# A decoder trunk of two layers: input laid out transposed, attention outputs stored already split

## The chip, the cores and the metric

The kernel runs on one core of one Trainium2 chip. The time is that of one execution on the device, in microseconds (us); where several runs are given, their median. A profile is one further execution, recorded by the hardware profiler: PE is TensorE (the matrix engine; PEld its weight loads), DVE VectorE, ACT ScalarE, POOL GpSimd, SP SyncE. SP, ACT and POOL also issue transfers (DMA), each in its own order; a trailing q (SPq) marks such a queue's work.

## The reference, cut to what matters

Two residual layers over 512 tokens of width 2048, all in float32.

```python
for i in range(DEPTH):                                  # DEPTH = 2
    hn = rms_norm(x, norm_w[i])
    if i % 2 == 0: out = diff_attention_mixer(hn, ...)  # layer 0
    else:          out, v_first = rwkv7_mixer(hn, ...)  # layer 1
    x = x + out

# layer 0: 8 heads, q and k as 2 x 128 a head, v and gate as 256
q, k, v, gate = split(h @ w_in, 4)                      # w_in: 2048 x 8192
q, k = rope(rms_norm(q, q_gain)), rope(rms_norm(k, k_gain))
a = softmax(q0 k0) - lam * softmax(q1 k1)               # causal
o = rms_norm(a @ v, subln_w) * (1 - lambda_init) * silu(gate)
out = o @ w_out                                         # w_out: 2048 x 2048
```

Layer 1 (RWKV-7) has a wide in-projection, a recurrent state per head that is computed in chunks, and an out-projection of the same size. Almost nothing of it is touched.

## The kernel before

**Split products.** Each float32 operand of a matmul is split into a rounded high part and the rest (names ending in H and L, or wh and wl). `mm3` (L119) multiplies a pair by three matmuls: H x H, H x L, L x H. `split_w` (L104 on ACT, L105 on DVE) makes wh and wl from a weight chunk of two K tiles, "K tile" being 128 of the 2048 channels that are summed over. wraw (the raw weights) has three buffers, wh and wl two each, so one chunk is split while PE uses the other. L561 are the same products in the form that heads 1 to 7 use, where sums of blocks save products.

**Layer 0, start.** x (tokens on partitions) is loaded on SP in slices of 128 or 256 channels, in an order by hand (`issue_after`, which puts an instruction behind another of the same engine), with the first weight tile on ACT's queue behind a load of the norm weights as 32 rows. These are turned by PE into columns (`load_rows`, L197, L199). `more` turns x's slices on PE, four transposes a K tile (L829) into PSUM, between the matmuls of `unit_tok`; `make_h` (L1059 on ACT, L1060 on DVE) scales the turned tile by the norm weights and splits it into one of the 16 K tiles hH, hL. 1/rms is applied later, from 16 squares of x on ACT (L841). Some matmuls of the identity (L796) run ahead of the first product. Tables for rope and lambda are made on DVE from small loads on SP.

**Layer 0, heads.** The unit of head h (h = 1 to 7) runs while the attention of head h - 1 goes along in it as a chain: after so many matmuls (`tick`) it issues its next step. `turn_y` ends it: the output block y (128 tokens x 256) is turned, scaled into yTh by two ACT operations (L410) and stored to the DRAM tensor yd (channels x tokens) by ACT's queue (L411). There are 28 of these; those of head 7 go straight into two K tiles (L416, L417).

**Layer 0, out-projection.** `split_rows` loads yd's first 14 row tiles on SP into yr (L458) and `split_row` splits each into a pair of the pool hp, which is where the in-projection's K tiles were (L448 on ACT, L449 on DVE). `unit_tok` uses them for the first two of four column blocks, while head 7's attention runs as a chain (L311: transposes of q and k). For the other two, `sum_forms` loads rows again, on POOL, into frow (L643) and forms sums of blocks (L649 on DVE), which are split into fS (L661 on ACT, L662 on DVE); `seven` multiplies them. `take` (L525) adds finished PSUM blocks on DVE. The same `split_rows` and `sum_forms` serve layer 1's out-projection, from the tensor yd2.

**Order.** The program is written with priorities (`high_priority`: weight splits and make_h ahead, steps of a chain further ahead), and the framework fixes each engine's order when it is built. Tiles with the same tag share buffers; a tile waits for the last reader of the one that was there.

Of the kernel before, what the change touches and what calls it, by code (L numbers as in the profile page):

```python
# [13 lines left out]
F32 = mybir.dt.float32  # L14
# [75 lines left out]
def split_w(g, parts, kg, cols, k0, raw=None, fine=False):  # L90
# [7 lines left out]
    for ks in [slice(k, k + 1) for k in range(kg)] if fine else [slice(0, kg)]:  # L98
        k = k0 + ks.start
        with ExitStack() as after:  # L100
            if raw is not None and parts and k < 4:
                for ins in g.made[k - 1] if k else [g.made_prm]:
                    after.enter_context(g.tc.issue_after(ins))
            nc.scalar.copy(hi[:, ks], raw[:, ks])  # L104
            nc.vector.tensor_sub(lo[:, ks], raw[:, ks], hi[:, ks].bitcast(F32))  # L105
# [54 lines left out]
def unit_tok(g, aH, aL, parts, cols, npp=NT, more=None, late=True):  # L160
# [6 lines left out]
    for k0 in range(0, KT, KG):  # L167
        raw, fine = g.first.pop(0) if g.first else (None, False)
        if fine:
            more(1, None)  # L170
        wh, wl = split_w(g, parts, KG, cols, k0, raw, fine)
# [3 lines left out]
        for i, (k, t) in enumerate(order):  # L175
            if more and (fine and i % 2 == 0 or i in (0, 2, 4)):
                more(1 + i // 2 if fine else k0 + (k + 1 + i % 4 // 2 if by_k else KG + i // 2), m)
            kk = k0 + k
            s = slice(t * P, (t + 1) * P)
            m = mm3(nc, pts[t][:, :cols], aH[kk][:, s], aL[kk][:, s], wh[:, k, :], wl[:, k, :],  # L180
                    kk == 0, kk == KT - 1, g)
    return pts


def fetch_rows(g, pieces, queue, tag="junk", bufs=2):
    t = g.tmpc.tile([P, P], F32, name="prow", tag=tag, bufs=bufs)
    for r0, n, ap in pieces:
        queue.dma_start(out=t[r0 : r0 + n, :], in_=ap)
    return t


def load_rows(g, pieces, rows, queue=None, t=None):

    nc = g.nc
    t = t or fetch_rows(g, pieces, queue)
    ps = g.ps.tile([P, 512], F32, name="prp", tag="pa", bufs=2)
    nc.tensor.transpose(ps[:, :rows], t[:rows, :], g.ident[:rows, :rows])  # L197
    o = g.const.tile([P, rows], F32, name=f"prm{pieces[0][2].tensor.name}")
    g.made_prm = nc.vector.tensor_copy(o[:], ps[:, :rows]).ins  # L199
    return o  # L200


def rope_tables(g, aps):
# [3 lines left out]
    nc.sync.dma_start(out=pos_i[:], in_=aps["positions"].rearrange("o (t p) -> (o p) t", p=P),)  # L207
# [3 lines left out]
    nc.sync.dma_start(out=inv[:], in_=aps["inv_freq"].partition_broadcast(P))  # L211
# [21 lines left out]
    for i, nm in enumerate(("da_q_gain", "da_k_gain")):  # L233
        gn = tmp.tile([P, P], F32, name="gain" + nm)
        nc.sync.dma_start(out=gn[:], in_=aps[nm][0].partition_broadcast(P))
# [8 lines left out]
def lambda_full(g, aps):  # L244
    nc = g.nc
    e = []
    for i in (1, 2):
        a = g.tmpc.tile([P, P], F32, name=f"lq{i}")
        b = g.tmpc.tile([P, P], F32, name=f"lk{i}")
        nc.sync.dma_start(out=a[:], in_=aps[f"da_lam_q{i}"][0].partition_broadcast(P))  # L250
        nc.sync.dma_start(out=b[:], in_=aps[f"da_lam_k{i}"][0].partition_broadcast(P))
# [90 lines left out]
def attention(g, h, qkT, qkL, sq, V, VL, G, gap, rows=None, keys=()):  # L342
# [58 lines left out]
    def turn_y(t):  # L401
# [5 lines left out]
        if rows is None:  # L407
            yT = w.tile([P, 2, P], F32, name="yTh", tag="yTh", bufs=1)
            for c in range(2):
                nc.scalar.activation(yT[:, c], pv[:, c], AF.Copy, scale=g.subw[:, c : c + 1])  # L410
            nc.scalar.dma_start(out=g.yd[h * 256 : (h + 1) * 256, ts].rearrange("(c p) t -> p c t", p=P), in_=yT[:])  # L411
            return
# [225 lines left out]
def sum_forms(g, src, i, rows, homes):  # L638
# [3 lines left out]
    for r, k0 in zip(rows, (i * KG, NS + i * KG)):  # L642
        nc.gpsimd.dma_start(out=r, in_=src[k0 * P : (k0 + KG) * P, :].rearrange("(k p) t -> p k t", p=P))  # L643
# [128 lines left out]
def layer0(g, aps):  # L772
# [3 lines left out]
    with ExitStack() as cx:  # L776
# [5 lines left out]
        def load_x(xt, cs, at):  # L782
            with tc.issue_after(g.last) if g.last else ExitStack():
                g.last = nc.sync.dma_start(
                    out=xt[:, :, at], in_=aps["x"][0, :, cs].rearrange("(t p) c -> p t c", p=P)).ins
# [13 lines left out]
        with tc.high_priority(offset=AHEAD):  # L799
            xs += [xp.tile([P, NT, 512], F32, name=f"x{cb}") for cb in range(4)]  # L800
            g.first += [(g.wraw.tile([P, 2, 512], F32, name="wraw", tag="wraw"), i == 0) for i in range(3)]
            at = lambda k, n: (xs[k // 4], slice(k * P, (k + n) * P), slice(k % 4 * P, (k % 4 + n) * P))
# [8 lines left out]
            load_x(*at(1, 1))  # L811
            load_first(0, slice(1, 2))
            load_x(*at(2, 1))
            load_first(2, slice(0, 2))
            load_x(*at(3, 1))
            load_x(*at(4, 2))
            load_first(4, slice(0, 2))
            for k in range(6, KT, 2):
                load_x(*at(k, 2))
# [3 lines left out]
        def more(n, m):  # L823
            for k in range(len(g.hH), min(n, KT)):
                ps = g.ps.tile([P, 512], F32, name="xT", tag="pa", bufs=2)
                cb, c0 = k // 4, k % 4 * P
                for t in range(NT):
                    with tc.issue_after(m.ins if m else warmed):
                        last = nc.tensor.transpose(ps[:, t * P : (t + 1) * P], xs[cb][:, t, c0 : c0 + P], g.ident[:])  # L829
# [892 lines left out]
```

## Time and profile before

| | |
|---|---|
| Runs before (median of 3) | 2156.53 us (2153.41 to 2157.34) |
| Profiled execution, its own time | 2158.04 us |
| Its span, first to last instruction | 2156.3 us |
| PE busy | 2118.2 us, 98% |
| DVE, ACT, POOL busy | 1604.7, 1137.2 and 357.5 us |
| Mean granted clock | 0.992 |
| Last `make_h` of layer 0 starts at | 962.9 us |

A row of a group gives line, engine, operation, output <- inputs, shapes and count, then busy time and the mean of one in ns, then the engine's idle time just before and what ended it. A row in order of time begins with start and length in us; the bracket holds the idle time before it and what released it. A row of waits gives total us, times, longest.

### The profile page before, as it was taken

The numbers are of one execution on the slowest core, as the hardware profiler recorded it, in microseconds if no ns is written. First come the engines' busy times: TensorE is split into PE (matmuls) and PEld (weight loads), VectorE is DVE, ScalarE is ACT, GpSimd is POOL, SyncE is SP. The second block draws the span as 40 slices with busy tenths as digits, with TensorE's granted clock in tenths as the row PEclk, the third lists the DMA queues.
The fourth block names the chain that finished last, engine by engine and source line by source line (L and its number), as shares of the span: only waits on it lengthen the run. The fifth ranks groups of instructions, "written<-read, shape, count | busy, mean of one in ns | idle before, by whom it ended". The sixth has DMA issues, their size and how long they took to land.

```text
span 2156.3 us, 34231 instructions
## 1 busy us (share of the span) xinstructions
PE 2118.2 (98%) x12008; PEld 1722.0 (80%) x12008; DVE 1604.7 (74%) x4091; ACT 1137.2 (53%) x2265; POOL 357.5 (17%) x720
## 2 busy tenths in 40 slices
PE   9999999999999999999999999999999999999999
PEld 8888888888888788878676887887888778777887
DVE  5997888878788884576667778877777788767645
ACT  6565555655556453355554555565555555645322
POOL 0010101011011100101222212222222122221001
PEclk9999999999999999999999999999999999999999
DMA  6566767677676756723222323323333232345565
GB/s 194 148 138 175 167 157 186 150 181 165 158 186 167 187 187 193 165 79 96 79 79 77 94 83 91 91 78 100 94 93 93 84 91 91 104 126 180 180 164 122
DMA packets 135953, 284.12 MB, mean 132 GB/s; under 512 B 47636, under 2 KB 63972, under 8 KB 135780
## 3 DMA queue, kind: packets, MB, share of 16 engines
q1 hardware_dynamic: 81296, 187.89, 27.5%
q0 software_dynamic: 21760, 75.77, 18.6%
q10 hardware_dynamic: 32724, 18.27, 2.8%
q8 instruction: 94, 1.54, 0.3%
q14 instruction: 79, 0.65, 0.1%
HBM read 261.89 MB, written 19.99 MB: 131 GB/s over the span
## 4 chain that ended last, share of the span: by engine, by line
PE 32%; DVE 14%; issue 4%; DMA 3%; ACT 2%; SPq 0%; POOL 0%; ACTq 0%; DVEq 0%; POOLq 0%
PE pp L119 19%; PE pt L119 5%; DVE tmpl L1331 3%; DVE Tm L1333 2%; DVE wl L105 2%; DMA td<-Tm 2%; DVE VS L1466 1%; PE gp L1267 1%; PE sm L1444 1%; PE sm L1462 1%; DMA TT<-td 1%; PE sm L1455 1%; PE px L1373 1%; PE px L1363 1%; DVE l L1216 1%
## 5 line engine op out<-in xcount | busy, mean ns | idle before, releaser
L105 DVE TENSOR_TENSOR wl<-wraw,wh 128x1024 fp32r<-128x1024 f32 (+2 forms) x305 | 371.1, 1217 | 224.4 <-ACT wh L104 210.3
L104 ACT CAST wh<-wraw 128x1024 fp32r<-128x1024 f32 (+2 forms) x305 | 318.3, 1044 | 333.8 <-PE pp L119 182.7
L119 PE MATMUL pp<-hH,wl 128*128 128x512 f32 x1024 | 416.3, 407 | 0.5 <-DVE wl L105 0.5
L119 PE MATMUL pp<-hL,wh 128*128 128x512 f32 x1024 | 415.9, 406 | 0.0
L119 PE MATMUL pp<-hH,wh 128*128 128x512 f32 x1024 | 413.5, 404 | 0.0
L119 PEld LDWEIGHTS pp<-hH,wh 128*128 128x128 f32 x1024 | 194.8, 190 | 36.0 <-issue 1.5
L119 PEld LDWEIGHTS pp<-hL,wh 128*128 128x128 f32 x1024 | 194.7, 190 | 35.1
L561 PE MATMUL pp<-wh,hH 128*128 128x512 f32 x560 | 221.6, 396 | 1.1 <-ACT wh L104 0.7
L119 PEld LDWEIGHTS pp<-hH,wl 128*128 128x128 f32 x1024 | 194.6, 190 | 33.4 <-DVE wl L105 0.9
L561 PE MATMUL pp<-wh,hL 128*128 128x512 f32 x560 | 218.7, 391 | 0.0
L561 PE MATMUL pp<-wl,hH 128*128 128x512 f32 x560 | 174.6, 393 | 0.0
L119 PE MATMUL pp<-wl,hH 128*128 128x512 f32 x372 | 146.1, 394 | 2.4 <-DVE wl L105 2.4
L119 PE MATMUL pp<-wh,hH 128*128 128x512 f32 x372 | 147.3, 397 | 0.8 <-DVE acc L525 0.8
L119 PE MATMUL pp<-wh,hL 128*128 128x512 f32 x372 | 146.5, 395 | 0.0
L1331 DVE SCALAR_TENSOR_TENSOR tmpl<-LT,Tm 128x60 f32<-128x60 f32 (+24 forms) x496 | 134.6, 271 | 10.9
L1450 POOL COPY SA<-VS 64x64 f32<-64x64 f32 x224 | 60.9, 272 | 459.7 <-DVE VS L1466 355.1
L561 PEld LDWEIGHTS pp<-wh,hH 128*128 128x128 f32 x560 | 105.2, 188 | 23.4 <-ACT G L265 1.3
L561 PEld LDWEIGHTS pp<-wh,hL 128*128 128x128 f32 x560 | 105.2, 188 | 21.2
L561 PEld LDWEIGHTS pp<-wl,hH 128*128 128x128 f32 x560 | 103.3, 188 | 21.6 <-DVE wl L105 0.5
L1333 DVE TENSOR_TENSOR Tm<-Tm,tmpl 128x60 f32<-128x60 f32 (+24 forms) x496 | 104.5, 211 | 11.2
L1457 ACT COPY VS<-sm 64x64 f32<-64x64 f32 x256 | 52.8, 206 | 64.2 <-PE sm L1455 59.3
L119 PEld LDWEIGHTS pp<-wl,hH 128*128 128x128 f32 x372 | 70.2, 189 | 16.0 <-DVE wl L105 2.7
(387 smaller groups left out, 4263.3 us busy)
## 6 DMA issues: line engine op xcount, KB each, us to landing
wraw<-in_rw_w_in_dram SPq DMA_DIRECT2D x128, 512.0 KB
wraw<-in_da_w_in_dram SPq DMA_DIRECT2D x92, 512.0 KB
wraw<-in_da_w_out_dram SPq DMA_DIRECT2D x26, 512.0 KB
wraw<-in_rw_w_out_dram SPq DMA_DIRECT2D x26, 512.0 KB
Ta<-in_da_w_in_dram POOLq DMA_DIRECT2D x21, 512.0 KB, 5.6
Tb<-in_da_w_in_dram POOLq DMA_DIRECT2D x21, 512.0 KB, 5.9
Tc<-in_da_w_in_dram POOLq DMA_DIRECT2D x21, 512.0 KB, 5.7
wraw<-in_da_w_in_dram POOLq DMA_DIRECT2D x21, 512.0 KB, 5.7
```

The lines of the kernel that those rows point to most:

```text
L104: nc.scalar.copy(hi[:, ks], raw[:, ks])
L105: nc.vector.tensor_sub(lo[:, ks], raw[:, ks], hi[:, ks].bitcast(F32))
L119: m = nc.tensor.matmul(out, a, b, start=s, stop=e, skip_group_check=skip)
L561: m = nc.tensor.matmul(out[t][:], x, wt[lo][:, k, :], start=first, stop=end and lo == 1 and k == KG - 1, skip_group_check=True)
L1216: nc.vector.tensor_tensor_scan(l[:].rearrange("p c t -> p (c t)"), g.rmask[:].rearrange("p c t -> p (c t)"), lw[:], 0.0, ALU.mult, ALU.add)
L1267: m = nc.tensor.matmul(gp[h][:, i * P : (i + 1) * P], BK[r_, c0 + i, :, :], p.AR[r_, c0 + i, :, :], start=True, stop=True)
L1331: nc.vector.scalar_tensor_tensor(tt, LT[:, i : i + 1, i + 1 :].to_broadcast([P, s, n]), n2[:, i : i + 1], Tm[:, 0:s, i : i + 1].to_broadca ...
L1333: nc.vector.tensor_add(Tm[:, 0:s, i + 1 :], Tm[:, 0:s, i + 1 :], tt)
L1363: nc.tensor.matmul(px[hi, c * HALF : (c + 1) * HALF], p.G[lo, c, 0, h, HALF:C], T1[lo, c, :], start=True, stop=True, tile_position=(b0, b0 ...
L1373: nc.tensor.matmul(px[lo, N + c * HALF : N + (c + 1) * HALF], X[hi, c, :], TT[hi, c, h, HALF:C], start=True, stop=True, tile_position=(b0 ...
L1450: nc.gpsimd.tensor_copy(p.SA[r_, c - 1, :], VS[r_, c, h, :])
L1457: nc.scalar.copy(VS[r_, c, h, :], sm[r_, P : P + C])
```

## The change

Five things. (1) The host also hands over x transposed, as xT with channels on partitions, and the norm weights and the RWKV constants as columns. `make_h` reads xT from SBUF; x itself is loaded later, for the squares, on ACT's queue. The hook is now `turn`, called by `split_w` after each split; `more` stays for the out-projections. Ten warm-up matmuls come ahead of the first product. (2) `rwkv_consts` loads three tensors as columns instead of rows that PE turns. (3) Small loads go on POOL instead of SP, and the mask is made on POOL first. (4) `turn_y` makes both parts of the output and stores them to yd, now of the shape (16, 128, 2, 512), in two stores; before the out-projection, the parts are loaded into tiles of hp with no split. (5) `sum_forms` loads yd's high part and adds the low part onto it with a second, adding load.

```diff
 def split_w(g, parts, kg, cols, k0, raw=None, fine=False, turn=None):
...
-            if raw is not None and parts and k < 4:
-                for ins in g.made[k - 1] if k else [g.made_prm]:
-                    after.enter_context(g.tc.issue_after(ins))
-            nc.scalar.copy(hi[:, ks], raw[:, ks])
-            nc.vector.tensor_sub(lo[:, ks], raw[:, ks], hi[:, ks].bitcast(F32))
+            for ins in g.made[-1] if turn and g.made else ():
+                after.enter_context(g.tc.issue_after(ins))
+            a = nc.scalar.copy(hi[:, ks], raw[:, ks])
+            d = nc.vector.tensor_sub(lo[:, ks], raw[:, ks], hi[:, ks].bitcast(F32))
+        if turn:
+            turn(ks.stop - ks.start, a.ins, d.ins)
...
 # turn_y
-            yT = w.tile([P, 2, P], F32, name="yTh", tag="yTh", bufs=1)
             for c in range(2):
-                nc.scalar.activation(yT[:, c], pv[:, c], AF.Copy, scale=g.subw[:, c : c + 1])
-            nc.scalar.dma_start(out=g.yd[h * 256 : (h + 1) * 256, ts].rearrange("(c p) t -> p c t", p=P), in_=yT[:])
+                yT = w.tile([P, 2, P], F32R, name="yTh", tag=("yTh", "th")[c], bufs=1)
+                nc.scalar.activation(yT[:, 0], pv[:, c], AF.Copy, scale=g.subw[:, c : c + 1])
+                nc.vector.scalar_tensor_tensor(yT[:, 1], pv[:, c], g.subw[:, c : c + 1],
+                                               yT[:, 0].bitcast(F32), ALU.mult, ALU.subtract)
+                nc.scalar.dma_start(out=g.yd[2 * h + c, :, :, ts], in_=yT[:].bitcast(F32))
...
 # sum_forms
-        nc.gpsimd.dma_start(out=r, in_=src[k0 * P : (k0 + KG) * P, :].rearrange("(k p) t -> p k t", p=P))
+        if len(src.shape) == 2:
+            nc.gpsimd.dma_start(out=r, in_=src[k0 * P : (k0 + KG) * P, :].rearrange("(k p) t -> p k t", p=P))
+            continue
+        for part, op in ((0, ALU.bypass), (1, ALU.add)):
+            nc.gpsimd.dma_start(out=r, in_=src[k0 : k0 + KG, :, part].rearrange("k p t -> p k t"),
+                                accum_op=op)
...
 # layer0, start
-            load_x(*at(0, 1))
-            warmed = warm_up(5)
-            g.prm_a = load_rows(g, [(0, 32, aps["norm_w"].rearrange("l (k p) -> (l k) p", p=P))], 32, nc.scalar)
-            first = load_first(0, slice(0, 1), nc.scalar)
+            g.prm_a = g.const.tile([P, 32], F32, name="norms")
+            first = nc.scalar.dma_start(out=xT[:, 0], in_=aps["xT"][:, 0]).ins
+            with tc.issue_after(first):
+                first = nc.scalar.dma_start(out=g.prm_a[:], in_=aps["norm_w"]).ins
+            g.last = load_w(g, g.first[0][0], qk_cols(aps, 0), 0, slice(0, 1), nc.sync)
+            warmed = warm_up(10)
...
-        def more(n, m):
-            for k in range(len(g.hH), min(n, KT)):
-                ps = g.ps.tile([P, 512], F32, name="xT", tag="pa", bufs=2)
-                cb, c0 = k // 4, k % 4 * P
-                for t in range(NT):
-                    with tc.issue_after(m.ins if m else warmed):
-                        last = nc.tensor.transpose(ps[:, t * P : (t + 1) * P], xs[cb][:, t, c0 : c0 + P], g.ident[:])
-                if k == 0:
-                    warm_up(7, last.ins)
-                with tc.high_priority(offset=AHEAD):
-                    g.made.append(make_h(g, ps, k))
+        def turn(n, a, d):
+            for k in range(len(g.hH), len(g.hH) + n):
+                with tc.high_priority(offset=AHEAD), tc.issue_after(a), tc.issue_after(d):
+                    g.made.append(make_h(g, xT[:, k], k))
+        qk0 = unit_tok(g, g.hH, g.hL, qk_cols(aps, 0), 512, turn=turn, behind=warmed)
...
+        for cb in range(4):
+            xs.append(xp.tile([P, NT, 512], F32, name=f"x{cb}"))
+            with tc.issue_after(g.made[min(2 * cb + 6, KT - 1)][0]):
+                nc.scalar.dma_start(out=xs[cb][:], in_=aps["x"][0, :, cb * 512 : cb * 512 + 512].rearrange(
+                    "(t p) c -> p t c", p=P))
...
-                with tc.issue_after(g.made[min(4 * cb + 4 + t, KT - 1)][0]):
+                with tc.issue_after(g.made[min(2 * cb + 11, KT - 1)][0]):
                     nc.scalar.activation(junk[:], xs[cb][:, t, :], AF.Square, accum_out=sc[:, t, cb : cb + 1])
...
 # layer0, before the out-projection
-        rows = split_rows(g, g.yd, ("t1",), 4, KT - 2, 8, g.gated)
+        rows = []
+        for k in range(KT - 2):
+            rows.append([g.hp.tile([P, T], F32R, name=n, tag=n) for n in ("hH", "hL")])
+            for i in range(2):
+                nc.sync.dma_start(out=rows[k][i][:].bitcast(F32), in_=g.yd[k, :, i])
...
 # rwkv_consts
-    tb, tm = [fetch_rows(g, x, nc.scalar, t, 1) for x, t in ((pbs, "at"), (mus_, "al"))]
...
+    with g.tc.issue_after(g.made[-1][0]):
+        for t, n in ((pb, "rw_cols"), (g.mu, "rw_mu_cols"), (g.mut, "rw_mu_lora")):
+            nc.scalar.dma_start(out=t[:], in_=aps[n])
...
-    g.yd = dr.tile([D, T], F32, name="yd")
+    g.yd = dr.tile([KT, P, 2, T], F32, name="yd")
```

More of the change, by code (lines that the diff above doesn't have):

```diff
@@ L157, in tick, with unit_tok @@
                 c.step(g)
-def unit_tok(g, aH, aL, parts, cols, npp=NT, more=None, late=True):
+def unit_tok(g, aH, aL, parts, cols, npp=NT, more=None, late=True, turn=None, behind=None):
     nc = g.nc
@@ L168, in unit_tok @@
         raw, fine = g.first.pop(0) if g.first else (None, False)
[L169 to L171 removed]
+        wh, wl = split_w(g, parts, KG, cols, k0, raw, fine, turn)
         by_k = fine or more and late and k0 + KG == KT
@@ L175, in unit_tok @@
         for i, (k, t) in enumerate(order):
-            if more and (fine and i % 2 == 0 or i in (0, 2, 4)):
-                more(1 + i // 2 if fine else k0 + (k + 1 + i % 4 // 2 if by_k else KG + i // 2), m)
+            if more and i in (0, 2, 4):
+                more(k0 + (k + 1 + i % 4 // 2 if by_k else KG + i // 2), m)
             kk = k0 + k
             s = slice(t * P, (t + 1) * P)
-            m = mm3(nc, pts[t][:, :cols], aH[kk][:, s], aL[kk][:, s], wh[:, k, :], wl[:, k, :],
-                    kk == 0, kk == KT - 1, g)
-    return pts
[L185 to L200, printed above, removed]
+            with g.tc.issue_after(behind) if behind and not m else ExitStack():
+                m = mm3(nc, pts[t][:, :cols], aH[kk][:, s], aL[kk][:, s], wh[:, k, :], wl[:, k, :],
+                        kk == 0, kk == KT - 1, g)
+    return pts
 def rope_tables(g, aps):
```

85 lines of the change are left out of this document (40 added, 45 removed).

## The prediction

> **What bounds the kernel now.** I read the page's shares first, then a table of stretches, then the waits of PE, and last the order of time at the three places that the change touches.
>
> ```profile
> span 2156.3 us, 34231 instructions
> PE 2118.2 (98%) x12008; PEld 1722.0 (80%) x12008; DVE 1604.7 (74%) x4091; ACT 1137.2 (53%) x2265; POOL 357.5 (17%) x720
> ```
>
> PE is busy 98% of the span, so only two things can move the time: PE instructions that go, and PE waits that go or come. In the stretches (us; then busy us and instructions of PE, PEld, DVE, ACT, POOL; granted clock; DMA share; GB/s):
>
> ```profile
> 2.00:24.00 22.00, 21.72 (x113) 18.54 (x114) 8.90 (x12) 11.40 (x19) 0.41 (x1) 1.00 1.06 341
> 24.00:58.35 34.35, 34.35 (x171) 28.42 (x170) 24.86 (x83) 23.70 (x51) 0.00 (x0) 1.00 0.34 102
> 120.00:700.00 580.00, 578.94 (x2786) 480.96 (x2787) 478.01 (x1270) 332.19 (x606) 66.76 (x80) 1.00 0.71 168
> 744.00:752.00 8.00, 3.37 (x14) 1.96 (x13) 7.45 (x26) 5.13 (x12) 0.00 (x0) 0.91 0.36 122
> 752.00:757.00 5.00, 5.00 (x16) 4.14 (x17) 1.73 (x6) 1.87 (x5) 0.00 (x0) 0.50 0.82 272
> 800.00:848.00 48.00, 48.00 (x213) 39.74 (x213) 25.93 (x35) 18.14 (x27) 1.42 (x2) 1.00 0.57 187
> ```
>
> The first unit (to 58.3) and heads 1 to 7 keep PE full. The one hole in layer 0 is 744 to 757, where head 7's in-projection hands over to the out-projection: PE idles 8.00 - 3.37 = 4.6 us and then runs 5 us at a granted clock of 0.50, another 2.5 us of full-speed work lost. What it waits for there:
>
> ```profile
> PE pp L119 <- DVE wl L105: 2.4, 1, 2.4
> PE pt L311 <- ACT t L296: 1.3, 1, 1.3
> PE pp L119 <- DVE acc L525: 0.8, 1, 0.8
> ```
>
> **The change part by part.**
>
> **1. The start: transposed input.** In order of time (start us, length, engine, line):
>
> ```profile
> 5.48 0.62 ACT L104 CAST wh<-wraw 128x512 fp32r<-128x512 f32 x1 [2.17 <-DMA wraw<-in_da_w_in_dram]
> 6.84 0.75 DVE L1060 SCALAR_TENSOR_TENSOR hL<-xT,prmin_norm_w_dram,hH 128x512 fp32r<-128x512 f32 x1
> 7.58 0.48 PE L119 MATMUL pp<-wh,hH 128*128 128x512 f32 x1
> 22.36 1.05 ACT L104 CAST wh<-wraw 128x1024 fp32r<-128x1024 f32 x1 [2.67 <-DMA wraw<-in_da_w_in_dram]
> 28.70 0.60 PE L829 MATMUL xT<-ident,x 128*128 128x128 f32 x4
> 35.09 0.60 PE L829 MATMUL xT<-ident,x 128*128 128x128 f32 x4
> 57.65 0.39 PE L119 MATMUL pp<-wh,hH 128*128 128x512 f32 x1
> 58.33 0.39 PE L119 MATMUL pp<-wh,hH 128*128 128x512 f32 x1
> ```
>
> The last two rows are three matmuls apart: 0.68 / 3 = 0.227 us each. From 28.70 to 35.09 is one chunk of two K tiles, 24 matmuls and two groups of four transposes: 6.39 - 24 x 0.227 = 0.94, so a group costs 0.47 us of PE. The unit has 16 tiles x 4 x 3 = 192 matmuls; from its first (7.58) to the next unit's first (58.33) are 50.75 us, of which 192 x 0.227 = 43.6 is matmuls and 7.1 the 15 groups. The change removes them all (the first, and the norm transpose of L197, lie before 7.58). The first matmul now needs one landing, one cast (0.62), one make_h pair and the ten warm-ups that it is put behind: the cast no longer waits for the norm row's turn, and the weights are first on their queue instead of second behind it. Today they land at 5.48; first in the queue, 1 to 1.5 us sooner is my estimate. With 0.62, 0.69 and 0.75 in a row hL is then ready at about 6.0 to 6.5; I take 6.0 for the first matmul (bounds 5.4 and the old 7.58). The unit then ends at 6.0 + 43.6 = 49.6 instead of 58.3: **-8.7**, between -9.3 and -7.1.
>
> What hides the rest (groups up to 58.3: count, busy us, mean ns, idle before).
>
> ```profile
> L1059 ACT ACTIVATE hH<-xT,prmin_norm_w_dram 128x512 fp32r<-128x512 f32 x16 | 11.0, 689 | 9.8 <-PE xT L829 9.7
> L841 ACT ACTIVATE junkx<-x 128x512 f32<-128x512 f32 x16 | 10.0, 624 | 0.1
> ```
>
> The weights of the fourth chunk stand in the queue behind all of xT and landed at 22.36 with the DMA engines full (share 1.06, 341 GB/s over 2 to 24). The bytes ahead are the same 6.3 MB (16 + 8 tiles of 262 KB): at 341 GB/s, from 2 us on, 20.5 us. PE asks for that chunk at 6.0 + 72 x 0.227 = 22.3, and cast plus subtract take some 1.3 us before the first matmul: just in time. If this cover goes (landing again 22.36) PE waits 22.36 + 1.3 - 22.3 = 1.4 us. x itself is loaded a second time, 4.2 MB in four issues on ACT's queue, behind made tiles 6 to 12, so after this landing; between 24 and 58 the DMA share is 0.34, and ACT is busy 23.7 of 34.35, which takes four issues in. The 16 squares stay. The nine small loads move from SP to POOL, which does nothing from 24 to 58 (x0), and only rope and lambda on DVE wait for them: 0. wh has two buffers, so the last chunk is cast when the sixth is done, 6.0 + 144 x 0.227 = 38.7; with 1.05 and twice 0.69 tile 15 is made at 41. ACT has the last eight squares behind it (0.62 and a short read each, some 6 us), so they end near 47, and the four copies that free PSUM for the next unit begin then: about 1.5 us before PE asks. 0, or up to +2 if that slips.
>
> **2. Constants.** Three transposes for rwkv_consts and eleven short loads on ACT become three loads.
>
> ```profile
> L197 PE MATMUL prp<-ident,prow x3: 259/272/311, 4.3 to 108.8; 32*128 32x32 f32 x1, 112*128 112x112 f32 x1, 64*128 64x64 f32 x1
> ```
>
> Two of these transposes and the one of mut are PE work of 0.1 to 0.3 us each: **-0.4** (0 to -1).
>
> **3. Heads 1 to 7: stores already split.** Count, duration in ns (min/median/max), first and last start:
>
> ```profile
> L410 ACT ACTIVATE yTh<-yt,subw x56: 358/364/371, 141.4 to 709.8; 128x128 f32<-128x128 f32 x56
> L411 ACTq DMA_DIRECT2D yd<-yTh x28: 366/366/446, 142.0 to 710.2; - x28
> L417 DVE SCALAR_TENSOR_TENSOR hL<-yt,subw,hH x8: 344/350/352, 777.4 to 796.9; 128x128 fp32r<-128x128 f32 x8
> 784.71 0.37 ACT L416 ACTIVATE hH<-yt,subw 128x128 fp32r<-128x128 f32 x1 [0.42 <-DVE hL L417]
> ```
>
> Each of 28 turn_y gains two DVE operations like L417 (56 x 0.35 = 19.6 us), one more issue on ACT (28 x 0.37 = 10.2 us), and a new wait: the store stands on ACT behind DVE's subtract, as L416 does (0.42). Queued behind it on ACT is the next weight cast, and PE waits for that. DVE has 580 - 478 = 102 us free there and ACT 248, so most of it hides. Bounds: 0, and all of the ACT part, 28 x (0.37 + 0.42) = 22. PE's whole idle time in this stretch is 580.00 - 578.94 = 1.1 us with 28 turn_y in it; doubling what a turn_y asks should at most double this: **+1.1**.
>
> **4. The hand-over at 744: rows loaded into the K tiles.**
>
> ```profile
> L449 DVE TENSOR_TENSOR hL<-yr,hH x28: 670/684/694, 751.3 to 1980.1; 128x512 fp32r<-128x512 f32 x28
> L448 ACT CAST hH<-yr x28: 601/616/628, 737.4 to 1978.1; 128x512 fp32r<-128x512 f32 x28
> 734.65 0.33 SPq L458 DMA_DIRECT2D yr<-yd  x1
> 748.07 1.22 DVE L105 TENSOR_TENSOR wl<-wraw,wh 128x1024 fp32r<-128x1024 f32 x1
> 749.34 1.20 PE L119 MATMUL pp<-wl,hH 128*128 128x512 f32 x4 [2.44 <-DVE wl L105]
> 749.35 1.95 SPq L78 DMA_DIRECT2D wraw<-in_da_w_out_dram  x2
> 759.27 1.05 ACT L104 CAST wh<-wraw 128x1024 fp32r<-128x1024 f32 x1
> ```
>
> Half of each group (14) is layer 0's: 8.6 us of ACT and 9.6 us of DVE go, all but the two casts at 737 and 744 after 751. The wl that PE waits for is made at 748.07 behind DVE work that stays (takes, VL, gates), so this wait does not end sooner. But today PE has only four hH x wh matmuls to do meanwhile, because the first hL row comes only at 751.3. With both rows landed, 16 matmuls (two tiles, four token blocks, hH and hL with wh) need no wl: 12 more before it, and four more wl ones right after, 16 x 0.227 = 3.6 us that fill idle time. The 2.5 us of low clock go if this keeps the clock, and stay if not; I take half, 1.2. **-4.8**, between 0 (the order of PE stays) and -7.1 (all of the hole).
>
> The loads: 28 of 256 KB on SP instead of 14. Rows 0 to 5 wait for the last use of those K tiles at about 734, as the first yr does; weights behind them wait too. Twelve pairs are 6.3 MB, 18.5 us at 341 GB/s, so until about 753, while PE needs a pair each 2.7 us from 744.5: 0. Late next: the weight loads issued at 749.35, the first of which is cast at 759.27.
>
> **5. The sums for the out-projection (frow).** Each of six loads on POOL becomes two, the second adding onto the first and so waiting for its landing, with POOL's later issues queued behind that wait.
>
> ```profile
> L643 POOL DMA_DIRECT2D frow<-yd x6: 707/718/726, 778.8 to 806.5; - x6
> DMA to landing us min/median/max: 4.5/6.3/7.8
> L649 DVE TENSOR_TENSOR frow<-frow x12: 681/685/693, 797.1 to 820.5; 128x512 f32<-128x512 f32 x12
> DVE frow L649 <- DMA frow<-yd: 3.6, 1, 3.6
> 809.03 1.22 DVE L105 TENSOR_TENSOR wl<-wraw,wh 128x1024 fp32r<-128x1024 f32 x1
> 813.18 1.05 ACT L104 CAST wh<-wraw 128x1024 fp32r<-128x1024 f32 x1 [2.21 <-PE pp L119]
> L119 PE MATMUL pp<-wh,fS x96: 388/392/398, 878.3 to 922.0; 128*128 128x512 f32 x96
> ```
>
> A group is then three landings in a row, 19 us: the first is complete at 798, the second at 812, the third near 826, against first uses at 797, 803 and 814 today. PE wants the results only at 878.3, so nothing is late for PE itself; the harm is in DVE's order, where wl splits may stand behind a frow operation that waits. Today's 3.6 us wait of this kind cost PE nothing (48.00 of 48.00 busy). Lower bound 0. Upper: waits of 9 and 15 us, each less the 3.1 us by which a wl runs ahead here (one ends at 810.2, and PE changes to its chunk at 813.2, when the next cast gets its buffer), are 18. Nearest is today's row, so I take **+2**. The weight additions at 848 are behind the third group on POOL: 22 us to spare.
>
> By the Trainium skill (DMA: Bandwidth & Descriptors, Anatomy of one DMA) a POOL transfer takes 2.0 us plus bytes / 436 GB/s, an estimate of 3.2 us for 512 KB and 9.6 us for the three in a row. That would take this term to 0; the trace's median of 6.3 us disagrees and decides.
>
> **Sum:** -8.7 - 0.4 + 1.1 - 4.8 + 2 = -10.8. The profiled execution took 2158.0 (span 2156.3 and 1.7 around it), 1.5 above the median of the runs, 2156.5; from the median this gives **2145.7**.
>
> **The rivals.**
> A, *the hand-over stays*: PE's order there is fixed at build time, and DVE is busy 7.45 of 8.00 with work that stays. Then only the start pays: 2145.7 + 4.8 = 2150.5. Against it: row data really are what the first hL matmuls wait for.
> B, *the start is bound by DMA*: the share is 1.06 until 22 and the same bytes come. The fourth chunk waits 1.4 us and the end slips by 2 for the squares: 2145.7 + 3.4 = 2149.1. Against it: from 24 on the queue is a third full.
> C, *slower, through POOL's chain of adding loads*: DVE stands at frow for the 9 and 15 us of part 5 and holds wl: +18 instead of +2, 2161.7. It decides from 12.8 us of PE wait on. For it: today's order already lets DVE run into a 3.6 us wait for one landing, and three landings come in place of one. Against it: 55 us of slack lets wl go first.
> D, *ACT's new wait in the heads*: 28 x 0.79 reaches PE, +22 instead of +1.1: 2166.6. Against it: ACT is busy only 332 of 580.
> E, *the clock stays full at the hand-over*: -7.1 there in full, 2143.4. The row at 752 shows 0.50 after a stretch with no gap above 2.44 us, so what counts is activity over some microseconds, and that rises.
> The skill (TensorE: Matmul & The Clock Gate, What's actually happening) says the gate watches a free-running window of some 3.4 us of activity. This trace agrees as far as 3.37 busy of 8.00 us was enough to lose half the clock; its other wording, an idle gap of that length, it does not bear out.
>
> **How the numbers follow.** My forecast 0.42, A 0.22, B 0.12, C 0.10, D 0.06, E 0.08. A measurement here tells about 0.2%, 4.3 us, from no change. Faster by more: forecast, E, and most of A and B, 0.78; C in half strength (+9, 2152.7) and weak mixtures of A and B lie within: 0.11; slower, C and D in force: 0.11. The range goes from all gains at their ends (-9.3 - 1 - 7.1 = -17.4, 2139.1, cut to 2140) to A with half of C, 2155. The likeliest case alone spans 2142 to 2150.
>
> **What would show it.** Right: no L829 in the first unit, its first matmul near 6 and the next unit's near 49.6; no L449 before the RWKV layer; 744 to 757, shifted, with more than 5 us of PE in the first 8. Wrong: PE waiting for wl between the hand-over and 848 with DVE idle at L649 in front; an ACT wh late behind a store in the heads; ACT waiting for wraw in the first 25 us.

## The result, and the profile after

The changed kernel takes 2185.1 us (median of 4; 2182.1 to 2198.2) against 2156.9 for the kernel before beside it: 1.0144 times as long, 95% interval 1.0114 to 1.0175. The prediction said 2145.7, a gain of 10.8; the kernel lost 28. The profiled execution has a span of 2185.2.

The page of the changed kernel, first part:

```profile
span 2185.2 us, 34215 instructions
PE 2118.4 (97%) x11936; PEld 1720.5 (79%) x11936; DVE 1608.0 (74%) x4129; ACT 1132.0 (52%) x2251; POOL 368.4 (17%) x735
```

PE has 72 instructions less and is busy as long as before (2118.2): the turns of x are gone, and as much busy time came back, at a mean granted clock of 0.985 where it was 0.992. Its stretches (columns as in the prediction):

```profile
2.00:24.00 22.00, 16.70 (x70) 13.08 (x70) 7.01 (x9) 8.36 (x12) 5.75 (x10) 0.96 0.97 270
24.00:58.95 34.95, 34.95 (x143) 28.22 (x142) 23.86 (x70) 20.50 (x37) 0.00 (x0) 0.93 0.74 263
120.00:700.00 580.00, 578.63 (x2766) 477.91 (x2766) 484.02 (x1308) 331.54 (x601) 65.76 (x79) 1.00 0.72 171
760.00:768.00 8.00, 5.05 (x15) 3.60 (x14) 5.76 (x19) 3.54 (x9) 0.00 (x0) 0.68 0.94 330
800.00:848.00 48.00, 33.76 (x146) 26.78 (x145) 20.00 (x43) 14.23 (x27) 7.79 (x8) 0.89 0.73 190
```

Two stretches that PE filled before have holes: the first unit (16.70 of 22, at 270 GB/s instead of 341), and the out-projection at 800 (33.76 of 48, before 48.00). The waits of PE, to 120 us and from 700 to 960:

```profile
PE pp L120 <- ACT t L247: 8.4, 1, 8.4
PE pp L120 <- ACT hH L1053: 5.2, 2, 4.7
...
PE pp L120 <- DVE wl L104: 18.5, 3, 9.0
PE pt L361 <- DVE yTh L393: 2.9, 1, 2.9
```

Five rows in the order of time cut every kernel here into the same stretches: the copies that free the first unit's banks (L265 before, L247 after), head 7's last in-projection product, the first product with fS, the first of lora (the start of layer 1's work, 932.6 in the kernel before; the `make_h` at 962.9 in the first table is already layer 1's), the end. Lengths in us from one profiled execution each; the last columns are medians of the runs and the ratio to the kernel before with its interval. The kernel before was run again beside each e, with medians of 2159.5 to 2160.3: the ratios compare, the bare times of two rows need not.

| kernel | copies at | heads | out-proj. 1 | out-proj. 2 | layer 1 | time | ratio |
|---|---|---|---|---|---|---|---|
| before | 57.1 | 687.2 | 134.0 | 54.3 | 1223.7 | 2156.9 | |
| changed | 66.7 | 692.5 | 152.8 | 54.2 | 1219.0 | 2185.1 | 1.0144 (1.0114 to 1.0175) |
| e1 start alone | 66.2 | 685.5 | 134.4 | 54.2 | 1217.4 | 2160.1 | 1.0007 (0.9996 to 1.0019) |
| e2 rows alone | 57.5 | 703.7 | 152.8 | 54.4 | 1219.2 | 2189.2 | 1.0146 (1.0116 to 1.0175) |
| e3 no adding load | 65.4 | 697.5 | 131.3 | 54.1 | 1221.2 | 2165.7 | 1.0030 (1.0010 to 1.0050) |
| e4 small loads on SP | 63.6 | 693.0 | 152.2 | 54.2 | 1221.7 | 2184.1 | 1.0115 (1.0094 to 1.0137) |
| e5 start, small on SP | 58.6 | 686.7 | 134.8 | 54.2 | 1220.6 | 2157.1 | 0.9994 (0.9978 to 1.0010) |
| e6 and squares early | 54.2 | 687.3 | 135.2 | 54.2 | 1221.4 | 2153.7 | 0.9972 (0.9955 to 0.9988) |
| e7 sums from SBUF | 65.7 | 693.3 | 132.3 | 54.2 | 1222.7 | 2172.2 | 1.0057 (1.0032 to 1.0081) |
| e8 all repairs | 54.1 | 695.6 | 131.0 | 54.1 | 1222.9 | 2159.8 | 1.0005 (0.9986 to 1.0024) |
| e9 squares earlier | 54.5 | 688.2 | 135.3 | 54.2 | 1222.1 | 2159.2 | 0.9995 (0.9978 to 1.0012) |
| e10 small on POOL, late | 58.4 | 685.3 | 134.9 | 54.2 | 1220.0 | 2155.3 | 0.9987 (0.9971 to 1.0003) |
| e11 low part only | 54.3 | 691.3 | 134.1 | 54.2 | 1213.9 | 2156.0 | 0.9988 (0.9967 to 1.0009) |
| e12 second store only | 54.1 | 693.2 | 137.3 | 54.2 | 1214.7 | 2159.9 | 1.0010 (0.9985 to 1.0034) |
| e13 copies before cast | 51.7 | 687.6 | 135.1 | 54.2 | 1227.8 | 2156.7 | 0.9989 (0.9973 to 1.0005) |
| e14 = e6 again | 54.2 | 687.4 | 134.4 | 54.1 | 1226.9 | 2157.0 | 0.9992 (0.9972 to 1.0011) |

So the loss is +9.6 at the start, +5.3 in the heads and +18.8 in the out-projection's first half; layer 1, whose instructions the change hardly touches, gave 4.7 back. The experiments are about these four numbers.

### The profile page after: what moved, and what is told of

Read it like the earlier page. It is cut to its first block, busy times and chain, and to the rows that moved or that the text cites. A ratio compares the mean times of both kernels' runs of the same rounds, so it can differ in the third digit from the quotient of the medians.

```text
span 2185.2 us, 34215 instructions
## 1 busy us (share of the span) xinstructions
PE 2118.4 (97%) x11936; PEld 1720.5 (79%) x11936; DVE 1608.0 (74%) x4129; ACT 1132.0 (52%) x2251; POOL 368.4 (17%) x735
## 4 chain that ended last, share of the span: by engine, by line
PE 31%; DVE 13%; issue 3%; DMA 2%; ACT 1%; POOL 0%; SPq 0%; ACTq 0%; DVEq 0%; POOLq 0%
PE pp L120 19%; PE pt L120 5%; DVE tmpl L1316 3%; DVE Tm L1318 2%; DVE wl L104 2%; DVE VS L1451 1%; DMA td<-Tm 1%; PE gp L1252 1%; PE sm L1429 1%; DMA TT<-td 1%; PE sm L1447 1%; PE sm L1440 1%; PE px L1358 1%; DVE l L1201 1%; PE px L1348 1%
## 5 line engine op out<-in xcount | busy, mean ns | idle before, releaser
L545 PE MATMUL pp<-wh,hL 128*128 128x512 f32 x560 | 219.7, 392 | 0.0
L545 PE MATMUL pp<-wl,hH 128*128 128x512 f32 x560 | 175.4, 395 | 0.3
L120 PE MATMUL pp<-wl,hH 128*128 128x512 f32 x372 | 151.6, 408 | 18.5 <-DVE wl L104 18.5
L120 PE MATMUL pp<-wh,hL 128*128 128x512 f32 x372 | 150.2, 404 | 0.1
L1316 DVE SCALAR_TENSOR_TENSOR tmpl<-LT,Tm 128x60 f32<-128x60 f32 (+24 forms) x496 | 134.8, 272 | 10.9
L545 PEld LDWEIGHTS pp<-wh,hH 128*128 128x128 f32 x560 | 105.6, 189 | 23.2 <-ACT wh L103 2.7
L120 PEld LDWEIGHTS pp<-wh,hH 128*128 128x128 f32 x372 | 72.5, 195 | 30.9 <-ACT t L247 8.8
```

The lines of the kernel that those rows point to most:

```text
L120: m = nc.tensor.matmul(out, a, b, start=s, stop=e, skip_group_check=skip)
L545: m = nc.tensor.matmul(out[t][:], x, wt[lo][:, k, :], start=first, stop=end and lo == 1 and k == KG - 1, skip_group_check=True)
L1316: nc.vector.scalar_tensor_tensor(tt, LT[:, i : i + 1, i + 1 :].to_broadcast([P, s, n]), n2[:, i : i + 1], Tm[:, 0:s, i : i + 1].to_broadca ...
```

## The experiments

**e1, e2: the two halves alone.** e1 keeps parts 1 to 3 and takes turn_y, the rows and the sums from the kernel before; e2 is the reverse.

> The kernel before with parts 1 to 3 of the change alone (transposed input, constants as columns, small loads on POOL); y is stored once and split after loading, as before. Theory S (the start is a loss of its own): in the trace of the changed kernel the second unit begins 9.0 us late (67.32 against 58.33) and runs at clock 0.50 until about 73, worth another 2.6. So 2156.5 + 11.6 = 2168, with the second unit's first matmul near 67. Rival (the start gains as predicted when it stands alone, and the late start comes from the order of the whole program, which the other parts shift): 2148 to 2152, second unit near 50.

> The kernel before with parts 4 and 5 alone (split stores, rows into the K tiles, adding loads); start and constants as before. Theory S: the two DVE waits for frow, each followed by a low clock, cost 20.4 (stretch from head 7's last in-projection matmul to the first fS matmul 152.8 against 134.0, with the hand-over 1.6 better), the wait for turn_y's bank about 4; 2156.5 + 20.4 + 4 - 1.6 = 2179 (2176 to 2182). Rival (the bytes, not the chain: the small loads and the x reload of the start are what delays everything later): 2152 to 2158.

The places were as the theory said (e1's copies at 66.2, e2's out-projection at 152.8); the totals were 8 less for e1 and 10 more for e2 than it gave. e1's late start is 9.1 and its layer 1 is 6.3 shorter; e2 lost 16.5 in the heads, of which 5.0 is idle time of PE at 166 to 186, where the changed kernel has 0.7. So both expected times were missed. "Same time" for e1 thus hides a loss, and e14 shows what hides it.

**e3, e7: the sums.** e3 leaves the second load out, and with it the low part; e7 loads nothing for the sums and adds hH and hL, which are in SBUF.

```diff
-        for part, op in ((0, ALU.bypass), (1, ALU.add)):
+        for part, op in ((0, ALU.bypass),):                      # e3
...
+        for k in range(KG):                                      # e7, no load
+            nc.vector.tensor_tensor(out=r[:, k], in0=tiles[k0 + k][0][:].bitcast(F32),
+                                    in1=tiles[k0 + k][1][:].bitcast(F32), op=ALU.add)
```

> The changed kernel with the adding load left out: frow gets the high part of y alone, so the low part is left out of the sums. Theory C (POOL's chain of adding loads): the two waits of PE for wl (9.0 each) and the low clock after them go, 2185.1 - 20.4 = 2165 (2162 to 2168), DVE's idle time in front of the frow operations below 5 us. Rival (DVE's order was merely built another way, with frow operations ahead of wl): waits stay at half or more, 2175 or above.

> The changed kernel, with frow made by 12 DVE additions from the K tiles hH and hL that are in SBUF already, and no frow loads. Theory C (the wait for landings is the loss, not the work): the two waits of 9 for wl go, at 12 x 0.69 = 8.3 us of DVE work that 22 of 48 free us cover; 2185.1 - 20.4 = 2165, as with the low part left out, or a little less since 6 MB of loads go. Rival (DVE gets too full and wl is late behind the additions): PE waits for wl of 5 us or more in 800 to 860, 2170 or above.

In the changed kernel, DVE and then PE in the order of time:

```profile
822.54 0.69 DVE L638 TENSOR_TENSOR frow<-frow 128x512 f32<-128x512 f32 x1 [11.78 <-DMA frow<-yd]
823.15 1.22 DVE L104 TENSOR_TENSOR wl<-wraw,wh 128x1024 fp32r<-128x1024 f32 x1
...
847.92 0.69 DVE L638 TENSOR_TENSOR frow<-frow 128x512 f32<-128x512 f32 x1 [11.54 <-DMA frow<-yd]
848.53 1.22 DVE L104 TENSOR_TENSOR wl<-wraw,wh 128x1024 fp32r<-128x1024 f32 x1
...
824.42 0.80 PE L120 MATMUL pp<-wl,hH 128*128 128x512 f32 x1 [9.00 <-DVE wl L104]
849.80 0.80 PE L120 MATMUL pp<-wl,hH 128*128 128x512 f32 x1 [6.75 <-DVE wl L104]
```

DVE stands 11.8 and 11.5 us in front of frow with a wl behind it, and PE stands 9.0 and 6.75 for that wl. What DVE waits for is on POOL:

```profile
792.22 2.13 POOL L631 DMA_DIRECT2D frow<-yd  x3 [61.08 <-PE sc L120]
797.04 1.21 POOL L631 DMA_DIRECT2D frow<-yd  x1 [2.69 <-DMA frow<-yd]
799.60 3.13 POOL L631 DMA_DIRECT2D frow<-yd  x3 [1.35 <-DMA frow<-yd]
816.17 1.18 POOL L631 DMA_DIRECT2D frow<-yd  x1 [13.45 <-DMA frow<-yd]
```

These eight loads fill four tiles, two groups. Three plain loads go out first, then the three that add onto them, and behind those, at 801.05, the fourth tile's plain load: it took 14.8 us to land, and the load that adds onto it (816.17) another 6.3. The first group was complete at 808.4, and DVE did not wait for it; the second, with the fourth tile, at 822.4. e7's waits of PE from 760 to 960 and of DVE for frow in e3:

```profile
PE pp L120 <- DVE wl L104: 2.7, 1, 2.7
```

```profile
DVE frow L638 <- DMA frow<-yd: 4.9, 1, 4.9
```

What is left in e7 is the wait at the hand-over; in e3 DVE still waits 4.9 for a single landing, and that costs PE nothing, as the 3.6 of before. Out-projection 1 goes from 152.8 to 131.3 and 132.3: the adding loads cost 20.5 to 21.5, DVE's additions in their place 1 at most. This is shown. How much of it is each load's wait for the one before it and how much the adding loads' own length, these two runs do not part. e3's time came as expected; e7's, 2172.2, was 7 above, without the wait of 5 us or more for wl that its rival asks for.

**e4, e5, e10: the small loads.** In e4 and e5 the nine small loads of rope, lambda and subw go out on SP behind the first weights (e4 in the changed kernel, e5 in the start alone, the one for subw first); in e10 they stay on POOL behind a short copy of the sixth hL.

```diff
-        nc.gpsimd.dma_start(out=gn[:], in_=aps[nm][0].partition_broadcast(P))   # and eight like it
+        nc.sync.dma_start(out=gn[:], in_=aps[nm][0].partition_broadcast(P))     # e4, e5
...
+            masked = nc.gpsimd.tensor_copy(held[:], g.hL[5][:, 0:64].bitcast(F32)).ins   # e10
```

> The changed kernel with the nine small loads back on SP's queue, behind the xT loads and the first weights (undoes part 3). Theory P (the small loads on POOL, out at 2.4 to 8.8 us, hold the DMA engines: full share at 92 GB/s from 10 to 12 us): the third chunk of weights is cast near 15 instead of 21.3, the fourth near 21 to 22 instead of 28.7, the first unit ends near 53; the squares' tail stays, so the second unit begins near 61 and the time is 2185.1 - 6 = 2179. Rival (the xT loads stand ahead of the weights and fill the engines by themselves): third chunk still at 20 or later, 2183 to 2187.

> The kernel before with parts 1 to 3, but the small loads on SP's queue behind the first weights (the one for subw in front of the others, since in the run before DVE stood 5.7 us for it). Theory P with a tail on ACT (the small loads on POOL starve the weights; and ACT makes the 16 squares after the last K tile, 0.755 each, with two table loads and the copies of the unit behind them): no PE wait until the unit ends near 51, squares until 58, second unit near 59 instead of 66.8, so 2160.1 - 8 = 2152. Rival (the squares wait for x itself, loaded a second time, not for ACT's order): squares end after 62, 2155 or more.

> Parts 1 to 3 alone (2160.1 so, second unit at 66.8; with the small loads on SP 2157.1 and 59.2), with the small loads on POOL but held until the sixth K tile is made, near 16 us. Theory Q (it is POOL's queue: 228 packets with 0.42 MB took 55% of the engines' time from 8 to 18 us): the same 5 us are taken later, from 17 on, the fourth chunk or the x reload is late, second unit at 62 or later. Rival (it is only the early time, when PE hung on every landing): second unit at 59 to 60, as on SP.

DMA queues from 8 to 18 us (packets, MB, share of 16 engines), e1 and then e5:

```profile
q0 software_dynamic: 228, 0.42, 55.2%
q1 hardware_dynamic: 419, 1.27, 41.0%
```

```profile
q1 hardware_dynamic: 1159, 4.12, 102.5%
```

In e1, 0.42 MB of small loads hold 5.5 of 10 us of all engines, and the weights and xT get 1.27 MB instead of 4.12 (the last with the first small loads in it). The casts of the third and fourth weight chunks wait for that in the changed kernel, and PE with them; in e5 PE runs through to the unit's end:

```profile
21.26 1.04 ACT L103 CAST wh<-wraw 128x1024 fp32r<-128x1024 f32 x1 [8.44 <-DMA wraw<-in_da_w_in_dram]
28.72 1.05 ACT L103 CAST wh<-wraw 128x1024 fp32r<-128x1024 f32 x1 [5.18 <-DMA wraw<-in_da_w_in_dram]
22.98 0.79 PE L120 MATMUL pp<-wh,hH 128*128 128x512 f32 x1 [4.70 <-ACT hH L1053]
```

```profile
50.44 0.39 PE L120 MATMUL pp<-wh,hL 128*128 128x512 f32 x1
59.21 0.80 PE L120 MATMUL pp<-wh,hH 128*128 128x512 f32 x1 [8.38 <-ACT t L247]
```

e10's second unit begins at 59.05: from POOL, but later, they do no harm, so theory Q fell. (e5's second unit came where it was expected; its time, 2157.1 for 2152, did not.) It is the time, not the queue: in the first 20 us PE hangs on every landing. In e4 the third and fourth casts came as theory P says or sooner (12.6 and 19.4), but the copies only 3.1 sooner, and the time, 2184.1, lies in the rival's range: DVE then stood for subw, whose load went out last of the nine, at 23.2, and PE 2.9 for the wl behind it:

```profile
32.92 0.17 DVE L848 TENSOR_SCALAR subw<-subw 128x2 f32<-128x2 f32 x1 [5.70 <-DMA subw<-in_da_subln_w_dram]
```

**e6, e9, e13: ACT's order.** e5's 8.4 us at the unit's end stay. In e6 the hook that makes K tiles asks for x from the eighth on and places the squares between the casts; e9 moves x and squares up by a chunk and puts the second unit's second cast behind the copies; e13 is e6 with only the latter.

```diff
+            for cb in {12: (0,), 14: (1,), 16: (2, 3)}.get(len(g.made), ()):   # e6; e9: 10, 12, 14, 16
+                    with tc.high_priority(offset=AHEAD), tc.issue_after(g.made[-1][0]):
+                        q = nc.scalar.activation(junk[:], xs[cb][:, t, :], AF.Square, ...)
+                g.made[-1] += (q.ins,)                                         # the next cast comes behind
...
+            if guard: after.enter_context(g.tc.issue_after(guard))             # e9, e13; guard: last copy
```

> As the run with the small loads on SP, with x asked for from the eighth K tile on and the squares placed between the last three weight chunks, ahead of the next cast. Theory (ACT's order alone makes the tail): the copies begin at the unit's end near 51, second unit at 51 to 53 and no clock lost there, 2160.1 - 15 = 2145 (2143 to 2149). Rival (squares ahead of the casts wait for x and delay the weights): PE waits for wh or hH between 30 and 45, second unit near 59 as without it, 2152.

> As the run with the squares between the chunks (2153.7), each group of four one chunk earlier, and the cast of the second unit's second chunk put behind the four copies that free the banks (in that run the copies stood behind three squares and a cast that waited for PE, and PE waited 4.1 us at 50.8 and ran at a lower clock after). Theory (ACT's order is all that is left of the start's loss): second unit at 51 with no wait, 2153.7 - 4.1 - 2.5 = 2147 (2144 to 2150). Rival (x lands too late for squares one chunk earlier, the casts slip): PE waits for hH or wh between 28 and 45, 2152 or more.

> The run with the squares between the chunks (2153.7), with only the cast of the second unit's second chunk put behind the four copies, so that the last three squares and the copies no longer stand behind a cast that waits for PE until 50.8. Theory (that order is the last 4.1 us of the start's loss, and moving x itself earlier was what cost the run with the squares one chunk earlier 6.4 us of PE waits between 28 and 45): second unit at 52 to 53, PE wait below 2.5 us, the clock kept, 2149 (2146 to 2152). Rival (nothing more is to be had at the start): 2153 or more, wait of 4 us as before.

ACT and DVE in the changed kernel: the first of the squares after the last K tile, the last one, the sum, the copies, and PE:

```profile
50.30 0.62 ACT L829 ACTIVATE junkx<-x 128x512 f32<-128x512 f32 x1
65.72 0.63 ACT L829 ACTIVATE junkx<-x 128x512 f32<-128x512 f32 x1
66.48 0.17 DVE L830 TENSOR_REDUCE ss<-ssc 128x4 f32<-128x16 f32 x1 [4.67 <-ACT junkx L829]
66.68 2.05 ACT L247 COPY t<-pp 128x512 f32<-128x512 f32 x4 [0.24 <-DVE ss L830]
67.32 0.80 PE L120 MATMUL pp<-wh,hH 128*128 128x512 f32 x1 [8.37 <-ACT t L247]
```

All but one of the squares stand behind the last K tile in ACT's order, with table loads and the next unit's casts among them, and the copies stand behind their sum. e6's row for the second unit has a wait of 4.1 (three squares behind a cast that waited for PE until 50.8), e13's 1.6:

```profile
54.86 0.80 PE L120 MATMUL pp<-wh,hH 128*128 128x512 f32 x1 [4.09 <-ACT t L247]
```

```profile
52.33 0.50 PE L122 MATMUL pp<-wh,hH 128*128 128x512 f32 x1 [1.59 <-ACT t L249]
```

That the order makes the tail is shown, step by step: second unit at 59.2, 54.9, 52.3. e9 lost again what it won, on x that landed too late for squares a chunk earlier (ACT 2.47 in front of one, then PE waits of 1.6 and 1.0 for hH): there the rival was right. PE's idle time in e9 from 28 to 45 is 2.6, not the 6.4 in e13's expectation. e13's PE is at lora 4.0 us earlier than before (928.6 against 932.6), yet its time cannot be told from before, and with it the expected 2149 failed.

**e11, e12: the split stores.** On e6's base, one adds DVE's low part (stored nowhere), the other a second store.

```diff
+                nc.vector.scalar_tensor_tensor(scrap[:, c], pv[:, c], g.subw[:, c : c + 1], yT[:, c], ...)   # e11
...
+            nc.scalar.dma_start(out=g.yd3[h * 256 : (h + 1) * 256, ts].rearrange(...), in_=yT[:])            # e12
```

> The run with the squares between the chunks (2153.7; from the copies at the first unit's end to head 7's last product 687.3 us), with one thing of the split stores: turn_y also makes the low part by two DVE operations, which is stored nowhere; nothing else changes. Theory B (DVE's second read holds the PSUM bank yt, behind DVE's other work): that stretch gets 5 to 8 us longer, as in the kernels with split stores (692.5 to 697.5 in four of the five), PE waits for pt behind this operation, 2159. Rival D (the stores themselves): 686 to 689, 2154.

> The same base with the other thing of the split stores: each block yTh is stored twice, the second time to a spare tensor, so ACT issues 28 stores more and twice the bytes leave; no DVE operation is added. Theory B: 686 to 689 us for that stretch, 2154. Rival D (ACT's scrap output of weigh's squares shares the buffer of yTh and waits for the store to land: 3.9 us at 706 in the changed kernel): ACT waits for landings of 3 us or more, the stretch gets 5 us or more longer, 2159.

The heads take 685.3 to 688.2 in all eight kernels with one store, 691.3 in e11 and 693.2 in e12, 692.5 to 703.7 in the six with split stores. Both halves cost, 4.0 and 5.9. Where, the order of time shows, in e11 and then in the changed kernel:

```profile
691.59 0.47 ACT L375 ACTIVATE junko<-o,r 128x256 f32<-128x256 f32 x1 [3.00 <-DMA yd<-yTh]
693.82 0.65 PE L361 MATMUL pt<-ident,a 128*128 128x128 f32 x4 [2.25 <-DVE scrap L394]
```

```profile
706.00 0.47 ACT L375 ACTIVATE junko<-o,r 128x256 f32<-128x256 f32 x1 [3.86 <-DMA yd<-yTh]
708.75 1.12 PE L361 MATMUL pt<-ident,a 128*128 128x128 f32 x4 [2.93 <-DVE yTh L393]
```

junko, weigh's scrap output, shares the one buffer of yTh, so ACT stands in front of it until the last store of yTh has landed. ACT's scaling of the next block and DVE's low part come behind it, and only then is the PSUM bank free that PE wants for pt. DVE's own part is small: in e11 it starts within 0.1 us of the end of ACT's. So it is rival D's wait that PE meets here, in e11 too, whose run was built for theory B. With the low clock after it (0.79 from 708 to 716 in the changed kernel) this one place is most of the loss: from head 6's first product with sumdd0H to head 7's are 91.0 us in the kernel before and in e6, 94.8 in e11 and 96.3 in the changed kernel.

In e12 ACT stands 2.6 in front of the same junko, for the semaphores of its two stores, and PE 0.9 behind it. Its casts also wait longer for weights: 31.1 us for landings from 120 to 735, in e6 18.1, with PE 1.7 behind four of them. PE's listed waits in the heads are 3.3 in all (0.9 in e6); how the second store costs the rest of 5.9 stays open.

**e8: all repairs in the changed kernel**, with weigh's scrap output in the unused half of its bank.

> The changed kernel with all repairs: small loads on SP, squares between the chunks, frow from SBUF, and the scrap output of weigh's squares in the unused half of its PSUM bank instead of the buffer yTh (so that ACT no longer waits for a store of yTh there, 3.9 us at 706). If the three losses add up: 2185.1 - 20.4 (sums) - 15 (start) - 4 (bank held by turn_y, and clock) = 2146 (2141 to 2151), below the kernel before. Rival (the split stores cost the heads more than that one wait): 2152 or more, with PE waiting for wh or yt behind stores in the heads.

2159.8: the rival. The start and the sums are repaired (54.1; 131.0), the heads are not (695.6). With junko out of the way, ACT's next yTh stands for the same store, and PE still waits 2.1 behind it:

```profile
695.73 0.37 ACT L391 ACTIVATE yTh<-yt,subw 128x128 fp32r<-128x128 f32 x1 [2.36 <-DMA yd<-yTh]
```

More buffers for yTh were not tried. Up to lora e8 is 3.9 behind e6, which has no split stores: the rows in the K tiles, with frow made from them, save some 4 in the out-projection (131.0 against 135.2), and their stores cost 8.3 in the heads (695.6 against 687.3).

**e14: e6 once more.**

> The run with the squares between the chunks once more, the same kernel, beside the kernel before. If its gain over the kernel before was real (2153.7 against 2159.5): ratio 0.997 again, its interval below 1. If it was the scatter of the runs (the kernel before spreads over 2150 to 2166): a ratio of 0.999 or more, with 1 in the interval.

The ratio came back as 0.9992 with 1 in its interval, so e6's gain is not established. Layer 1, the same kernel in two executions (e6, then e14):

```profile
930.90:2152.30 1221.40, 1193.12 (x7653) 959.25 (x7652) 877.46 (x2243) 631.85 (x1352) 262.37 (x597) 0.99 0.36 103
```

```profile
930.10:2157.00 1226.90, 1199.92 (x7653) 964.20 (x7652) 877.14 (x2243) 631.08 (x1352) 262.37 (x597) 0.98 0.35 103
```

The same 7653 matmuls are busy 6.8 us longer at a lower granted clock, while DVE, ACT and POOL are busy alike. So stretches of 1214 to 1228 in layer 1 say nothing of a change in layer 0, the 4.7 that the changed kernel "won" there included. No version here beats the kernel before beyond doubt; e13 is the shortest up to layer 1.

## Why the prediction was wrong

*Part 5, the sums: rival C, with a chance of 0.10, is what happened.* Both bounds had been worked out (0 and 18), and the wait was described as it came. The step that failed is the choice between them: "Nearest is today's row, so I take +2". Today's row was a wait of 3.6 for one landing with a wl far enough ahead; its price of zero says nothing about waits three times as long, and DVE's came at 11.8 and 11.5 where the bound had 9 and 15. The landings themselves were not later than said: from the first issue the first group was complete after 16.2 us and the second after 30.2, where 19 and 33 had been worked out. The order on POOL was another, plain loads of both groups first. The cost was 9.0 + 6.75 of PE's waits, near the bound of 18, and with the low clock after each, which no bound counted, 20.5 to 21.5. The estimate from the Trainium skill (DMA: Bandwidth & Descriptors, Anatomy of one DMA), 9.6 us for three loads in a row, is far below the 16.2 us of the first group, which had two in a row and the other group's loads beside it: here the measurement decides.

*Part 1, the start: the chain of products was right, two covers were not.* First matmul 6.46 (6.0 said); in e5 and e10, where PE does not wait in the unit, its first matmul starts at 6.43 and 6.48 and its last at 50.44 and 50.24, some 44 us (43.6 said). The first failed step is "only rope and lambda on DVE wait for them: 0" for the small loads: it asked who waits for them and not what they take from 16 engines while PE hung on every landing. Rival B had the DMA as the bound, but through xT, which in e5 came at 412 GB/s, weights included. The second is "0, or up to +2" for the squares: it let half of the squares run before the last K tile and counted ACT's time; ACT's order has 15 of the 16 after it. Nine us of lead became nine us of lag.

*Part 3, the heads: right sign, too small.* +1.1 said, +5.3 measured. The new wait that was priced is ACT's for DVE's subtract; the one that came is ACT's for the store's landing, since the buffer of yTh has a next user. It and the low clock after it were not in the rule "doubling what a turn_y asks should at most double this". D's own mechanism, wh late, cost 0.8.

*Part 4, the hand-over: right, too large.* PE was busy 5.05 of the first 8 us (more than 5 said), but the clock fell again (0.68), as in before, so E fell. Without the sums' loss, out-projection 1 is 1.7 to 3.0 shorter than before, where 4.8 was said.

*Part 2* (-0.4) is below what these runs can tell and was not tried alone.

*Only two things can move the time*, instructions of PE and its waits, said the first paragraph. The granted clock is a third, and the sum counted it at the hand-over alone: here it fell after each new wait (0.93 from 24 to 59, 0.89 from 800 to 848).

## What to carry to other kernels

A wait that the change adds to an in-order queue is priced by what stands behind it: find that instruction in the order and take the upper bound, until a row shows a wait of that length that cost nothing. For small transfers ask when they run, not only who waits for them; in a stretch where the matmuls hang on every landing, 0.4 MB cost 8 us here (copies at 66.2 in e1, 58.4 in e10). A buffer that a store reads is not free until the store has landed: ask who needs it next. Work "with room on its engine" is hidden only if the order puts it into that room.

## What the runs showed of the hardware

- An adding load takes more of the DMA engines than a plain one. The queue of the frow loads, 790 to 850 in the changed kernel and 775 to 830 in the kernel before:

```profile
q0 software_dynamic: 2496, 6.29, 46.2%
```

```profile
q0 software_dynamic: 864, 3.15, 17.3%
```

46.2% of 60 us is 27.7 us of all engines, 17.3% of 55 is 9.5: if the plain loads took that here too, the second, adding 3.14 MB took 18.2, about twice as much.
- Transposed x and weights, in pieces of 2 KB and more, load at 412 GB/s (8 to 18 us, e5); x in pieces of 512 bytes to 1 KB, also with weights, at 354 in the same window before.
- This kernel's time scatters by some 15 us between executions, and mostly with the granted clock: over 31 runs of the kernel before (2150.4 to 2166.1 us, mean clock 0.997 to 0.989) the two are correlated at -0.92.
- PE's clock fell to half after a single wait of 2.25 us (e11, 693.82): PE was busy all of 680 to 690, and from 694.8 to 698.2 the granted clock was 0.50 and a matmul took 0.63 us instead of 0.39.
